# Constant fills on GpSimd, maxima of pairs as a reduction, and a planner with other delays, in a hybrid encoder layer

## The chip, the cores and the metric

The kernel runs on one core of one Trainium2 chip. The metric is the device time of one execution in microseconds (us). The core has five instruction queues that each run in order: TensorE (PE, with its weight loads shown apart as PEld), VectorE (DVE), ScalarE (ACT), GpSimd (POOL) and SyncE (SP, which here only issues DMAs). They meet through semaphores. Matmul results lie in eight PSUM banks of 128 x 512 f32.

## What is computed

One encoder layer over 1024 tokens of width 1024, in float32: two attention groups side by side, an output projection, and a gated feed-forward net (FFN) with a short convolution. Cut to what matters:

```python
hn = rms_norm(x, norm1_g)
proj = hn @ w_in                       # -> qa (512) | ka, va (128 each) | qb, kb, vb (512 each)
qa = apply_axial_rope(rms_norm(qa, qa_norm_g), tables)
ka = apply_axial_rope(rms_norm(ka, ka_norm_g), tables)
out_a = global_gqa_attention(qa, ka, va)             # 8 query heads, 2 key heads, dense softmax
out_b = dilated_mixture_attention(rms_norm(qb, qb_norm_g), rms_norm(kb, kb_norm_g), vb)
mixed = concat([rms_norm(out_a, outa_norm_g), rms_norm(out_b, outb_norm_g)])
x = x + mixed @ w_out
x = x + conv_ffn(rms_norm(x, norm2_g), w_up, conv_w, conv_b, w_down)
```

Mixer B's `dilated_mixture_attention` attends through three windows, (128, 1), (512, 4) and (2048, 16) as (width, step), with a distance penalty for each head.

## The kernel before

Numbers are kept as pairs of fp32r (a rounded value and the remainder), so most products are three matmuls, and most operands are made by a copy on ACT and a subtraction ("split") on DVE.

**Stages.** (1) Up to about 187 us: the projections, as 28 products `in_product(m)`, m = 0 to 27, four chunks of seven Strassen-like products. `w_prep(m)` (L694) makes the weights of a product, on DVE a sum and a split; `in_out(m)` adds the result to its chunk. Queries of mixer A go through the steps of `done`: `square`, `root` (with the four small instructions of `newton`), `norm`, `table` and four `turn`s of two rotations each on GpSimd, then `cos` and `add` on DVE. (2) Up to about 405 us: mixer A, 16 groups g of 128 queries by four heads (`a_prep(g)`, `a_main(g)`). (3) Up to about 545 us: mixer B, 8 heads h (`b_prep(h)`, `b_s`, `b_pv`). (4) The output projection, to about 566 us. (5) The FFN.

**The maxima.** The softmax subtracts a maximum over all the keys of a query. `mx(i)` in `a_prep` makes scores of one query block in two banks of PSUM by two matmuls; DVE reduces each bank to a column, into `SM_MC` + i for the first half and `SM_MC` + 8 + i for the second. `last` takes the larger of each pair for the four i at once, writes it into spare columns of the query's remainder, and PE turns these round by four transposes, with a copy by ACT behind. `trl(hf)` in `b_prep` does the same for mixer B. So there are 32 such 128x4 instructions, 16 in each mixer.

**The hand-over.** The first group's maxima (`a_prep(0)`: `nat`, `first`, four `mx`, `last`) are computed between the last products, 25 to 27, on two banks used in turn. So the matmuls of the second `mx` wait for the reductions of the first.

**Constants.** Columns of the operand tiles hold constants: ones and zeros in `R_VA` and `R_VB` beside the values, zeros in `R_QLN` and `R_QLB`, −1 in the lower half of `R_KHA` and of one key set. Before, each is filled by a DVE `tensor_scalar` that multiplies any finite tile by 0 and adds the constant; there are 18 instructions, from `fill` (L538), `fill_k` (L674) and the list `fills`.

**What sets the order.** No engine's order is the code's. The class `Recorder` (L124) notes each operation, finds its dependencies, and gives it a cost (`price`). `simulate` then runs the program with these costs as a list scheduler: at each step it takes the engine that can start first, and on it the ready operation with the most urgent due time, PE's operations by their number in the code. A PSUM bank is held until the last user's end and delay. DVE instructions with two SBUF operands (and copies and `tensor_scalar` within SBUF) and GpSimd's share a lock in this model: one waits for the other. `emit` issues the operations in the order of their planned starts; each engine's queue then has this order fixed. As every instruction is issued in `emit`, every row of the profile names L437 (L442 in the changed kernel).

Of the kernel before, what the change touches and what calls it, by code (L numbers as in the profile page):

```python
# [11 lines left out]
F32 = mybir.dt.float32  # L12
# [3 lines left out]
OP = mybir.AluOpType  # L16
# [107 lines left out]
class Recorder:  # L124


    TABLE = {"Sqrt": 1, "Exp": 2, "Gelu_apprx_tanh": 3}

    def __init__(self, nc):
# [182 lines left out]
    def simulate(self, order=None, window=400):  # L312

        n = len(self.ops)
        eng = [op[0] for op in self.ops]
        succs = [[] for _ in range(n)]
        for i, p in enumerate(self.preds):
            for j in p:
                succs[j].append(i)
        lag = lambda i, j: (120 if self.short[i] else 0) if eng[i] == eng[j] != 4 and self.ops[i][1] != "dma_start" else \  # L320
            self.cost[i][1] + (self.cost[i][3] if self.ops[i][1] == "dma_start" else 0)
        late = [0.0] * n
        nxt = 0.0
        for i in range(n - 1, -1, -1):
            c = self.cost[i][0]
            t = min([late[j] - lag(i, j) for j in succs[i]], default=0.0) - c
            if eng[i] == 0:
                t = min(t, nxt - c)
                nxt = t
            late[i] = t  # L330
        key = [float(i) if eng[i] == 0 else late[i] + (self.cost[i][3] if eng[i] == 4 else 0) for i in range(n)]
        if order is not None:
            key = order
        left = [len(p) for p in self.preds]
        ready = [0.0] * n
        avail = [[] for _ in range(5)]
        for i in range(n):
            if not left[i]:
                avail[eng[i]].append(i)
        free = [700.0] * 5  # L340
        held = [[0.0] * 5 for _ in range(8)]
        lock = fabric = 0.0
        table = 0
        start, done = [0.0] * n, 0
        seq = []
        queue = None
        if order is not None:
            queue = [sorted([i for i in range(n) if eng[i] == e], key=lambda i: order[i]) for e in range(5)]
            head = [0] * 5
        lowest = 0  # L350
        waiting = [False] * n
        issued = [False] * n
        pe = [i for i in range(n) if eng[i] == 0]
        pe_at = 0

        def when(e, j):
            t = max(free[e], ready[j], lock if self.cost[j][2] else 0.0)
            for b in self.banks[j]:
                for k in range(4):
                    if k != e and held[b][k] > t:  # L360
                        t = held[b][k]
            return t

        while done < n:
            best = None
            for e in range(5):
                if queue is not None:
                    if head[e] < len(queue[e]) and not left[queue[e][head[e]]]:
                        i = queue[e][head[e]]
                        t = max(free[e], ready[i])  # L370
                        if best is None or t < best[0]:
                            best = (t, e, i)
                    continue
                a = avail[e]
                if not a:
                    continue
                t = min(when(e, i) for i in a)
                if best is None or t < best[0]:
                    best = (t, e, None)
            t, e, i = best  # L380
            if i is None:
                a = [j for j in avail[e] if when(e, j) <= t + 1e-6]
                i = min(a, key=lambda j: key[j])
                if e == 0:
                    while issued[pe[pe_at]]:
                        pe_at += 1
                elif e != 4:
                    soon = [j for j in avail[e] if t < when(e, j) < t + self.cost[i][0] and key[j] < key[i]]
                    if soon:
                        j = min(soon, key=lambda j: when(e, j))  # L390
                        if key[i] - key[j] > 2 * (when(e, j) - t):
                            i, t = j, when(e, j)
            c = self.cost[i]
            if c[2]:
                t = max(t, lock)
            for b in self.banks[i]:
                t = max(t, *[held[b][k] for k in range(4) if k != e])
            if e == 1 and c[3] and c[3] != table and self.ops[i][1] == "activation":
                t += 1290
                table = c[3]  # L400
            start[i] = t
            issued[i] = True
            free[e] = t + c[0]
            if c[2]:
                lock = t + c[0]
            end = t + c[0]
            if self.ops[i][1] == "dma_start":
                fabric = max(end + 600, fabric) + c[3]
                land = fabric + c[1] - 600
            else:  # L410
                land = end + c[1]
            for b in self.banks[i]:
                held[b][e] = land
            seq.append(i)
            done += 1
            if queue is None:
                avail[e].remove(i)
            else:
                head[e] += 1
            for j in succs[i]:  # L420
                same = eng[j] == e and e != 4 and self.ops[i][1] != "dma_start"
                ready[j] = max(ready[j], end + (120 if self.short[i] else 0) if same else land)
                left[j] -= 1
                if not left[j] and queue is None:
                    avail[eng[j]].append(j)
        self.start, self.late = start, late
        return seq, max(free)
# [13 lines left out]
def tile_encoder_layer(ctx, tc, x, xt, w_kv, w_in, gains, outg, norm2_g, w_out, w_up, conv,  # L441
# [95 lines left out]

    def fill(dst, n, m, c):  # L538

        vec.tensor_scalar(dst, f(O_IDF, m)[:, None, :].to_broadcast([128, n, m]), 0.0, c, op0=OP.mult, op1=OP.add)  # L540

# [129 lines left out]

    def fill_k():  # L674
        for i in range(4):
            vec.tensor_scalar(r(R_KHA + 512 * i, 512)[64:128], f(F_ROPE, 512)[64:128], 0.0, -1.0,
                              op0=OP.mult, op1=OP.add)


    def w_buf(c, half):  # L680
# [209 lines left out]
    def a_prep(g):  # L890
# [17 lines left out]
                vec.tensor_reduce(f(SM_MC + 8 * hf + i, 1), bank(t), axis=AX.X, op=OP.max)  # L908

        def last():  # L910
            vec.tensor_tensor(rp(R_QLN + 512 * kv + 64, [128, 4]), f(SM_MC, 4), f(SM_MC + 8, 4), op=OP.max)
            t = next_tr()
            for i in range(4):
                tr_r(t, i, r(R_QLN + 128 * (4 * kv + i), 128))
# [89 lines left out]
    def b_prep(h):  # L1004
# [43 lines left out]

        def trl(hf):
            qln = R_QLB[h % 2]  # L1050
            vec.tensor_tensor(rp(qln + 64 + 512 * hf, [128, 4]), f(SM_MC + 4 * hf, 4), f(SM_MC + 8 + 4 * hf, 4),
                              op=OP.max)
            t = next_tr()
            for i in range(4):
# [185 lines left out]
            fills.append(lambda o=R_VB + 1024 * i + c, v=v: fill(rp(o, [256, 4], [1, 64]), 4, 64, v))  # L1240
    fills.append(lambda: fill(rp(R_QLB[1] + 64, [128, 8], [1, 64]), 8, 64, 0.0))
    for i in range(4):
        fills.append(lambda o=R_SET[0] + 2048 + 512 * i: vec.tensor_scalar(
            r(o, 512)[64:128], f(O_QAB, 512)[64:128], 0.0, -1.0, op0=OP.mult, op1=OP.add))

    def take(prep, n):
        for _ in range(n):
# [533 lines left out]
```

## Time and profile before

| | us |
|---|---|
| median of 3 runs (1293.58 to 1294.5) | 1294.02 |
| the profiled execution, its own time | 1292.44 |
| its span in the trace | 1290.7 |
| idle time of PE in the span | 20.7 |
| DVE busy | 1104.3 |
| ACT busy | 739.1 |
| POOL busy | 106.7 |

How to read the rows: an instruction's row has its start, its length, the engine, the operation, the tile written and the tiles read (`bigf` the f32 arena, `bigr` the fp32r arena, `ps` PSUM) and their shapes; in brackets stands the engine's idle time just before it, and what ended that. A group's row has the count, the busy time in us and the mean in ns, and behind the second bar the idle time before its members. The chain is followed back from the last instruction to what released each step.

### The profile page before, as it was taken

What the parts mean: (1) busy time and instruction counts of PE and PEld (TensorE: products, weight loads), DVE (VectorE), ACT (ScalarE), POOL (GpSimd) and SP (SyncE); (2) the same over time, 40 slices, a digit from 0 to 9 for tenths busy, and PEclk for the clock granted to TensorE, in tenths of its full rate; (3) what the DMA queues carried; (4) which work ended last, traced back from release to release, by engine and by line L of the source; (5) the groups of instructions that cost most, each with busy time, mean ns of one, the idle gap of its engine ahead of it and who ended that gap; (6) DMA issues with size and microseconds to landing.
All of it is one profiled execution on the core that took longest, in us unless ns stands there. A gap on an engine that the chain in (4) does not pass through costs nothing.

```text
span 1290.7 us, 19118 instructions
## 1 busy us (share of the span) xinstructions
PE 1270.0 (98%) x6916; PEld 1083.5 (84%) x6916; DVE 1104.3 (86%) x1924; ACT 739.1 (57%) x1192; POOL 106.7 (8%) x99
## 2 busy tenths in 40 slices
PE   7999989999999999999999999999999999999998
PEld 7999987887888888878888888888888888888887
DVE  6997799999997778798589999999999998876664
ACT  7865456998888767763455444444444444343331
POOL 0011042301101212000130000000000000000000
PEclk9999999999999999999999999999999999999999
DMA  8534211100003643452313223323322337976873
GB/s 333 176 75 115 83 39 42 31 1 1 9 1 93 150 117 92 119 180 98 98 61 103 90 75 115 115 97 123 119 79 81 122 139 255 329 262 220 278 244 108
DMA packets 118206, 156.99 MB, mean 122 GB/s; under 512 B 50656, under 2 KB 75744, under 8 KB 117088
## 3 DMA queue, kind: packets, MB, share of 16 engines
q1 hardware_dynamic: 116816, 152.36, 36.8%
q0 software_dynamic: 1152, 3.15, 0.9%
q8 instruction: 54, 0.88, 0.3%
q10 hardware_dynamic: 144, 0.27, 0.1%
q14 instruction: 40, 0.33, 0.1%
HBM read 117.73 MB, written 33.82 MB: 117 GB/s over the span
## 4 chain that ended last, share of the span: by engine, by line
PE 89%; DVE 7%; ACT 2%; DMA 1%; issue 1%; DVEq 0%; ACTq 0%; SPq 0%
PE ps L437 89%; DVE bigf L437 4%; DVE bigr L437 3%; ACT bigf L437 1%; ACT bigr L437 1%; DMA bigf<-w_in 0%; DMA bigf<-w_kv 0%; DMA bigf<-w_out 0%; ACT L437 0%; ACT ps L437 0%; DVEq L437 0%; ACTq L437 0%; SPq L437 0%
## 5 line engine op out<-in xcount | busy, mean ns | idle before, releaser
L437 PE MATMUL ps<-bigr 128*128 128x512 f32 (+3 forms) x6532 | 1239.3, 350 | 15.7 <-ACT bigr L437 6.6
L437 PEld LDWEIGHTS ps<-bigr 128*128 128x128 f32 x6532 | 1044.8, 187 | 188.8 <-ACT bigr L437 11.6
L437 ACT ACTIVATE bigr<-bigf 128x512 fp32r<-128x512 f32 (+2 forms) x358 | 270.6, 769 | 291.1 <-PE ps L437 217.9
L437 DVE TENSOR_TENSOR bigr<-bigf,bigr 128x512 fp32r<-128x512 f32 (+2 forms) x326 | 283.3, 880 | 49.5 <-ACT bigr L437 46.0
L437 DVE TENSOR_TENSOR bigf<-bigf 128x512 f32<-128x512 f32 (+3 forms) x298 | 216.4, 749 | 25.2 <-DMA bigf<-w_down 18.4
L437 DVE TENSOR_TENSOR bigf<-ps,bigf 128x512 f32<-128x512 f32 (+3 forms) x262 | 177.6, 686 | 47.4 <-PE ps L437 37.5
L437 ACT ACTIVATE bigr<-ps 128x512 fp32r<-128x512 f32 (+1 forms) x292 | 166.9, 602 | 84.5 <-PE ps L437 82.9
L437 ACT ACTIVATE bigf<-bigf 128x1024 f32<-128x1024 f32 (+5 forms) x186 | 142.6, 794 | 74.9 <-DVE bigf L437 58.4
L437 DVE SCALAR_TENSOR_TENSOR bigf<-bigf 128x255 f32<-128x255 f32 (+6 forms) x283 | 164.0, 596 | 9.0 <-ACT bigf L437 5.5
L437 DVE TENSOR_TENSOR bigr<-ps,bigr 128x512 fp32r<-128x512 f32 x188 | 126.9, 684 | 27.1 <-ACT ps L437 17.8
L437 ACT ACTIVATE ps<-ps 128x512 f32<-128x512 f32 x192 | 115.1, 601 | 9.2 <-PE ps L437 8.3
L437 ACT ACTIVATE bigf<-ps 128x512 f32<-128x512 f32 (+3 forms) x112 | 71.1, 637 | 68.1 <-PE ps L437 42.8
L437 DVE TENSOR_REDUCE bigf<-ps 128x1 f32<-128x512 f32 x128 | 81.3, 680 | 1.9 <-PE ps L437 1.7
L437 POOL TENSOR_TENSOR bigf<-bigf 128x128 f32<-128x128 f32 (+3 forms) x54 | 58.2, 1104 | 255.8 <-DVE bigf L437 255.5
L437 POOL TENSOR_TENSOR bigr<-bigf,bigr 128x512 fp32r<-128x512 f32 x32 | 43.9, 1376 | 288.3 <-ACT bigr L437 124.4
L437 PE MATMUL ps<-bigf 65*128 65x65 f32 (+2 forms) x384 | 62.8, 293 | 1.1 <-DVE bigf L437 1.1
L437 PEld LDWEIGHTS ps<-bigf 65*128 65x128 f32 (+2 forms) x384 | 43.7, 139 | 14.0 <-DVE bigf L437 1.9
L437 DVE CUSTOM_DVE_ANT_1 bigf<-ps,bigf 128x432 bf16<-128x432 f32 x64 | 38.6, 603 | 3.4 <-PE ps L437 3.0
L437 DVE CUSTOM_DVE_ANT_0 bigf<-ps,bigf 128x256 bf16<-128x256 f32 x64 | 26.9, 420 | 2.9 <-PE ps L437 2.4
L437 DVE TENSOR_REDUCE bigf<-bigf 128x16 f32<-128x1024 f32 x13 | 15.8, 1213 | 1.2 <-ACT bigf L437 1.2
L437 ACT ACT_TABLE_LOAD x11 | 14.1, 1283 | 1.7 <-PEq L1773 1.2
L437 DVE TENSOR_SCALAR bigr<-bigf 128x256 fp32r<-128x256 f32 (+2 forms) x22 | 8.7, 427 | 5.2 <-DMA bigf<-w_kv 5.1
(18 smaller groups left out, 66.9 us busy)
## 6 DMA issues: line engine op xcount, KB each, us to landing
bigf<-w_down SPq DMA_DIRECT2D x99, 256.0 KB, 3.9
bigf<-w_up SPq DMA_DIRECT2D x44, 512.0 KB, 3.6
bigf<-gscr SPq DMA_DIRECT2D x77, 256.0 KB, 3.8
gscr<-bigf SPq DMA_DIRECT2D x33, 512.0 KB, 3.9
bigf<-w_in SPq DMA_DIRECT2D x8, 1024.0 KB, 6.1
bigf<-x SPq DMA_DIRECT2D x16, 512.0 KB, 4.7
bigf<-tmx SPq DMA_DIRECT2D x8, 672.0 KB, 4.1
bigr<-bigr SPq DMA_DIRECT2D x16, 256.0 KB, 3.0
```

The costliest lines, as they stand in the source:

```text
L437: method(*args, **kw)
```

## The change

1. `fill`, `fill_k` and the four lambdas of `fills` become GpSimd memsets: 18 instructions leave DVE and 18 come on GpSimd.
2. `last` and `trl` take the maxima of pairs by `tensor_reduce` over one operand whose inner axis strides from the first half to the second, in place of `tensor_tensor` over two operands.
3. The planner's delays between engines come from a table `LAG` (rows PE, ACT, DVE, GpSimd; columns the waiting engine, SP last), where each engine had one figure; a bank's holder releases it after the delay to the engine that waits. Where two engines could start at the same time, the one whose operation is more urgent is planned first, which decides who takes the lock.

The number of operations is the same.

```diff
+    LAG = ((215, 200, 200, 200, 195), (150, 150, 140, 185, 157), (135, 122, 140, 168, 115), (150, 150, 150, 150, 80))
...
-        lag = lambda i, j: (120 if self.short[i] else 0) if eng[i] == eng[j] != 4 and self.ops[i][1] != "dma_start" else \
-            self.cost[i][1] + (self.cost[i][3] if self.ops[i][1] == "dma_start" else 0)
+        is_dma = [op[1] == "dma_start" for op in self.ops]
+
+        def lag(i, j):
+            if is_dma[i]:
+                return self.cost[i][1] + self.cost[i][3]
+            if eng[i] == eng[j]:
+                return 120 if self.short[i] else 0
+            return self.LAG[eng[i]][eng[j]]
...
-                    if k != e and held[b][k] > t:
-                        t = held[b][k]
+                    if k != e and held[b][k] + self.LAG[k][e] > t:
+                        t = held[b][k] + self.LAG[k][e]
...
-                t = min(when(e, i) for i in a)
-                if best is None or t < best[0]:
-                    best = (t, e, None)
-            t, e, i = best
+                t, k = min((when(e, i), key[i]) for i in a)
+                if best is None or (t, k) < best[:2]:
+                    best = (t, k, e, None)
+            t, _, e, i = best
...
-        vec.tensor_scalar(dst, f(O_IDF, m)[:, None, :].to_broadcast([128, n, m]), 0.0, c, op0=OP.mult, op1=OP.add)
+        gp.memset(dst.bitcast(F32), c)
...
-            vec.tensor_scalar(r(R_KHA + 512 * i, 512)[64:128], f(F_ROPE, 512)[64:128], 0.0, -1.0,
-                              op0=OP.mult, op1=OP.add)
+            gp.memset(rf(R_KHA + 512 * i, 512)[64:128], -1.0)
...
-            vec.tensor_tensor(rp(R_QLN + 512 * kv + 64, [128, 4]), f(SM_MC, 4), f(SM_MC + 8, 4), op=OP.max)
+            vec.tensor_reduce(rp(R_QLN + 512 * kv + 64, [128, 4]), fp(SM_MC, [1, 4], [8, 2]), axis=AX.X, op=OP.max)
...
-            vec.tensor_tensor(rp(qln + 64 + 512 * hf, [128, 4]), f(SM_MC + 4 * hf, 4), f(SM_MC + 8 + 4 * hf, 4),
+            vec.tensor_reduce(rp(qln + 64 + 512 * hf, [128, 4]), fp(SM_MC + 4 * hf, [1, 4], [8, 2]), axis=AX.X,
                               op=OP.max)
...
-        fills.append(lambda o=R_SET[0] + 2048 + 512 * i: vec.tensor_scalar(
-            r(o, 512)[64:128], f(O_QAB, 512)[64:128], 0.0, -1.0, op0=OP.mult, op1=OP.add))
+        fills.append(lambda o=R_SET[0] + 2048 + 512 * i: gp.memset(rf(o, 512)[64:128], -1.0))
```

Where instructions move. First DVE at the hand-over, before: the tail of a root with `newton` (RECIPROCAL to SCALAR_TENSOR_TENSOR) around the split of the weights of product 27, `norm`, fills (TENSOR_SCALAR), the sum of product 25 (`ps,bigf`, 128x1024), a split of values, a fill, and the reductions of the first two `mx`.

```order
L437 RECIPROCAL bigf<-bigf 128x16
L437 TENSOR_TENSOR bigf<-bigf 128x16
L437 TENSOR_TENSOR bigr<-bigf,bigr 128x1024
L437 SCALAR_TENSOR_TENSOR bigf<-bigf 128x16 x2
L437 TENSOR_TENSOR bigf<-bigf 128x4x256
L437 TENSOR_SCALAR bigr<-bigf 128x4x64 x2
L437 TENSOR_SCALAR bigr<-bigf 128x8x64
L437 TENSOR_SCALAR bigr<-bigf 128x4x64 x2
L437 TENSOR_TENSOR bigf<-ps,bigf 128x1024
L437 TENSOR_TENSOR bigr<-bigf,bigr 128x8x64
L437 TENSOR_SCALAR bigr<-bigf 128x8x64
L437 TENSOR_REDUCE bigf<-ps 128x1 x4
```

The same place now. The first row is the sum of the weights of product 27, `cos` and `add`; then come the sum of product 24, the split of the weights of product 27, the first group's `nat`, the sum of product 25, the reductions, and behind them the root's tail, `v_scale`, another `nat` and `newton`.

```order
L442 TENSOR_TENSOR bigf<-bigf 128x4x256 x3
L442 TENSOR_TENSOR bigf<-ps,bigf 128x4x256
L442 TENSOR_TENSOR bigr<-bigf,bigr 128x1024
L442 TENSOR_TENSOR bigr<-bigf,bigr 128x4x64
L442 TENSOR_TENSOR bigf<-ps,bigf 128x1024
L442 TENSOR_REDUCE bigf<-ps 128x1 x4
L442 SCALAR_TENSOR_TENSOR bigf<-bigf 128x16
L442 TENSOR_TENSOR bigf<-bigf 128x8x64 x2
L442 TENSOR_TENSOR bigr<-bigf,bigr 128x4x64
L442 RECIPROCAL bigf<-bigf 128x16
L442 TENSOR_TENSOR bigf<-bigf 128x16
L442 SCALAR_TENSOR_TENSOR bigf<-bigf 128x16 x2
```

What moved: `cos`, `add` and the sum of product 24 stood behind the four reductions and stand ahead of them; `newton`, `norm`, `v_scale` and the split of values stood ahead and stand behind; the fills are gone from this queue.

GpSimd at the same place, before: eight rotations (128x8x16) of one block of queries, `table` and eight rotations of the next, `table` of a third, then the `v_split` and the two table loads for mixer B.

```order
L437 TENSOR_TENSOR bigf<-bigf 128x8x16 x8
L437 TENSOR_TENSOR bigf<-bigf 128x4x128
L437 TENSOR_TENSOR bigf<-bigf 128x8x16 x8
L437 TENSOR_TENSOR bigf<-bigf 128x512
L437 TENSOR_TENSOR bigr<-bigf,bigr 128x8x64
L437 DMA bigr<-tbc 128x768 x2
```

And now, from behind the first eight rotations:

```order
L442 MEMSET bigr 64x512 x3
L442 TENSOR_TENSOR bigf<-bigf 128x4x128
L442 MEMSET bigr 64x512
L442 TENSOR_TENSOR bigf<-bigf 128x8x16 x8
L442 MEMSET bigr 128x4x64 x4
L442 TENSOR_TENSOR bigf<-bigf 128x512
L442 MEMSET bigr 128x8x64 x3
L442 TENSOR_TENSOR bigr<-bigf,bigr 128x8x64
L442 MEMSET bigr 64x512 x2
L442 MEMSET bigr 128x8x64 x2
L442 MEMSET bigr 64x512 x2
L442 DMA bigr<-tbc 128x768 x2
```

The rotations and splits keep their order among themselves, the memsets stand between them, four of them ahead of the second eight rotations (one more stands ahead of the first eight) and all of them ahead of the table loads.

In mixer B the order of DVE around a `trl` stays; only the instruction is another. Before (the ISA rows are reductions of scores by a custom instruction and the read of its result, the RECIPROCAL belongs to an output):

```order
L437 ISA bigf<-ps,bigf 128x256
L437 ISA bigf 128x1
L437 TENSOR_TENSOR bigr<-bigf 128x4
L437 RECIPROCAL bigf<-ps 128x4
L437 TENSOR_TENSOR bigr<-ps,bigr 128x512
```

And now:

```order
L442 ISA bigf<-ps,bigf 128x256
L442 ISA bigf 128x1
L442 TENSOR_REDUCE bigr<-bigf 128x4
L442 RECIPROCAL bigf<-ps 128x4
L442 TENSOR_TENSOR bigr<-ps,bigr 128x512
```

Nothing moved here beyond the maximum's own operation.

More of the change, by code (lines that the diff above doesn't have):

```diff
@@ L371, in simulate @@
                         if best is None or t < best[0]:
-                            best = (t, e, i)
+                            best = (t, 0.0, e, i)
                     continue
@@ L396, in simulate @@
             for b in self.banks[i]:
-                t = max(t, *[held[b][k] for k in range(4) if k != e])
+                t = max(t, *[held[b][k] + self.LAG[k][e] for k in range(4) if k != e])
             if e == 1 and c[3] and c[3] != table and self.ops[i][1] == "activation":
@@ L406, in simulate @@
             end = t + c[0]
-            if self.ops[i][1] == "dma_start":
+            land = end
+            if is_dma[i]:
                 fabric = max(end + 600, fabric) + c[3]
                 land = fabric + c[1] - 600
-            else:
-                land = end + c[1]
             for b in self.banks[i]:
-                held[b][e] = land
+                held[b][e] = end
             seq.append(i)
@@ L420, in simulate @@
             for j in succs[i]:
-                same = eng[j] == e and e != 4 and self.ops[i][1] != "dma_start"
-                ready[j] = max(ready[j], end + (120 if self.short[i] else 0) if same else land)
+                ready[j] = max(ready[j], land if is_dma[i] else end + lag(i, j))
                 left[j] -= 1
```

## The prediction, made before the changed kernel was run

> **What bounds the kernel now.** I read the profile's engine line first, then its chain, the chain in order of time, and engine time cut by stage.
>
> ```profile
> PE 1270.0 (98%) x6916; PEld 1083.5 (84%) x6916; DVE 1104.3 (86%) x1924; ACT 739.1 (57%) x1192; POOL 106.7 (8%) x99
> PE 89%; DVE 7%; ACT 2%; DMA 1%; issue 1%; DVEq 0%; ACTq 0%; SPq 0%
> 565.82 719.00 PE ps L437 x3226
> ```
>
> PE is busy 1270.0 of 1290.7 us and carries the chain except at a few places. No PE instruction is removed, so only the 20.7 us in which PE idles, and steps that run slowly beside them, can be won. The stage table says where they are (columns: length; busy time with instructions of PE, PEld, DVE, ACT and POOL; granted PE clock; DMA share; GB/s):
>
> ```profile
> 187.00:209.00 22.00, 17.49 (x107) 14.59 (x106) 20.57 (x33) 6.05 (x11) 1.26 (x2) 0.92 0.28 82
> 209.00:405.00 196.00, 195.93 (x985) 158.42 (x984) 184.43 (x359) 174.15 (x328) 32.74 (x30) 1.00 0.06 12
> 405.00:545.00 140.00, 135.90 (x1007) 119.95 (x1006) 111.77 (x347) 102.25 (x188) 27.76 (x25) 1.00 0.49 124
> 545.00:566.00 21.00, 19.89 (x112) 15.68 (x111) 19.48 (x38) 14.47 (x25) 0.00 (x0) 1.00 0.55 175
> 566.00:1285.00 719.00, 719.00 (x3228) 594.75 (x3227) 607.95 (x929) 320.99 (x456) 17.28 (x12) 1.00 0.43 146
> ```
>
> PE idles 22.00 − 17.49 = 4.51 us at the hand-over from projections to mixer A, 0.07 in mixer A, 4.10 in mixer B, 1.11 at the hand-over to the FFN, and nothing in the FFN's 719 us. The rest lies in the load at the start and in the last 5.7 us, where the change touches nothing. Two places can move: 187 to 209, and mixer B.
>
> **The hand-over to mixer A.** The timeline of PE, and the group of its weight loads from 186 to 209:
>
> ```profile
> 185.74 1.62 PE L437 MATMUL ps<-bigr 128*128 128x256 f32 x10
> 190.84 7.50 PE L437 MATMUL ps<-bigr 128*128 128x512 f32 x35 [3.48 <-DVE bigf L437]
> 198.98 0.38 PE L437 MATMUL ps<-bigr 128*128 128x256 f32 x1 [0.64 <-DVE bigf L437]
> L437 PEld LDWEIGHTS ps<-bigr 128*128 128x128 f32 x112 | 15.8, 203 | 7.5 <-DVE bigf L437 5.8 <-ACT bigr L437 0.5 <-DVE bigr L437 0.4
> ```
>
> PE stands 3.48 us before the second pair of mx matmuls: their two banks hold the first pair, which DVE has not reduced. DVE in that stretch:
>
> ```profile
> 177.07 0.68 DVE L437 TENSOR_TENSOR bigr<-bigf,bigr 128x256 fp32r<-128x256 f32 x1
> 177.76 0.59 DVE L437 TENSOR_SCALAR bigr<-bigf 64x512 fp32r<-64x512 f32 x1
> 178.36 0.34 DVE L437 SCALAR_TENSOR_TENSOR bigf<-bigf 128x16 f32<-128x16 f32 x1
> 178.63 1.55 DVE L437 TENSOR_TENSOR bigf<-bigf 128x512 f32<-128x512 f32 x2
> 180.21 1.78 DVE L437 TENSOR_SCALAR bigr<-bigf 64x512 fp32r<-64x512 f32 x3
> 182.02 0.25 DVE L437 RECIPROCAL bigf<-bigf 128x16 f32<-128x16 f32 x1
> 182.31 0.87 DVE L437 TENSOR_TENSOR bigf<-bigf 128x16 f32<-128x16 f32 x1
> ...
> 184.24 1.48 DVE L437 SCALAR_TENSOR_TENSOR bigf<-bigf 128x16 f32<-128x16 f32 x2
> 185.75 1.22 DVE L437 TENSOR_TENSOR bigf<-bigf 128x1024 f32<-128x1024 f32 x1
> 186.90 1.23 DVE L437 TENSOR_SCALAR bigr<-bigf 128x256 fp32r<-128x256 f32 x5
> ...
> 189.17 0.68 DVE L437 TENSOR_TENSOR bigr<-bigf,bigr 128x512 fp32r<-128x512 f32 x1
> 189.77 0.42 DVE L437 TENSOR_SCALAR bigr<-bigf 128x512 fp32r<-128x512 f32 x1
> 190.11 1.28 DVE L437 TENSOR_REDUCE bigf<-ps 128x1 f32<-128x512 f32 x2
> ```
>
> DVE never rests here, and the reduces start at 190.11 behind ten fills (the TENSOR_SCALAR rows): 0.59 + 1.78 + 1.23 + 0.42 = 4.02 us, which leave DVE. By the new order the root's tail, v_scale, newton, norm and a v split also go behind the reduces: 0.34 + 1.55 + 0.25 + 0.87 + 1.48 + 1.22 + 0.68 = 6.4. Ahead of them come cos, add and the sum of product 24, by this group's mean 3 × 1.22 = 3.7:
>
> ```profile
> L437 DVE TENSOR_TENSOR bigf<-bigf 128x1024 f32<-128x1024 f32 x68 | 82.3, 1223 | 0.7
> ```
>
> And cos waits for GpSimd's eight rotations:
>
> ```profile
> 158.51 3.67 POOL L437 TENSOR_TENSOR bigf<-bigf 128x128 f32<-128x128 f32 x8 [31.95 <-DVE bigf L437]
> 174.75 8.40 POOL L437 TENSOR_TENSOR bigf<-bigf 128x128 f32<-128x128 f32 x9 [6.58 <-DVE bigf L437]
> ```
>
> This is the wait that the change adds, and everything on DVE queues behind it, the reduces included. Beside DVE's additions nine of these took 8.40 us; beside a DVE that reduces or waits, eight took 3.67, 0.46 each. In the new order DVE still has two additions until 177.1, under which I let two rotations pass; then it waits, so the other six take 6 × 0.46 = 2.8 and end at 179.9. From there cos, add, sum 24, split 27 and sum 25 (5 × 1.22), with a quarter-size split (0.3 to 0.68), end at about 186.4. The reduces start 3.7 us earlier; the same by difference: −4.0 − 6.4 + 3.7 + 2.8 = −3.9.
>
> What PE gets: the first reduce ends near 187.1 and PE is through with its ten matmuls at 187.36, so of 3.48 I leave 0.4 for ScalarE's copy: **−3.1**. Sum 24 is done before the last product, so the 0.64 at 198.98 goes: **−0.6**. Of the other 0.39 of idle half: **−0.2**. The granted clock of 0.92 cost 8% of 17.49, 1.4 us; with the long pause gone I count back half to two thirds: **−0.8**. Together −4.7. Bounds: 4.51 + 1.4 = 5.9, with 0.6 more for slow weight loads, is −6.5 at best; if the rotations end at 181.7 as in the run before and a contended DVE step comes on top, 2.2 us go back: −2.5.
>
> Newton and norm, put behind, are late next; they feed the next block of queries, well behind the first scores. The fills that DVE gives up stand on GpSimd, which had this to offer for a price:
>
> ```profile
> L437 POOL MEMSET bigf<- 128x8 f32 x1 | 0.1, 113 | 0.1
> L437 POOL TENSOR_TENSOR bigr<-bigf,bigr 128x512 fp32r<-128x512 f32 x32 | 43.9, 1376 | 288.3 <-ACT bigr L437 124.4 <-ACT bigf L437 59.8 <-PE ps L437 54.4
> ```
>
> A memset of 512 is between 0.11 (of 8 elements) and 1.38 us (a 512-wide subtraction with two operands). I take 0.7, half of the subtraction's row, which is the nearest in size and streams two operands that a memset has not. GpSimd idles 6.58 us ahead of the rotations, and the four memsets put there take 0.4 to 5.5: cost nothing on the sum. Queued behind the later ones are the v split and two table loads, wanted in mixer B, 200 us on.
>
> **Mixer B.** The 32 pair maxima cost 0.17 us each, except here (all DVE instructions of that form in mixer B: min, median, max in ns):
>
> ```profile
> L437 DVE TENSOR_TENSOR bigr<-bigf x14: 166/167/1279, 414.8 to 535.5; 128x4 fp32r<-128x4 f32 x14
> 456.86 1.26 POOL L437 TENSOR_TENSOR bigr<-bigf,bigr 128x512 fp32r<-128x512 f32 x1 [7.11 <-PE ps L437]
> 456.86 1.28 DVE L437 TENSOR_TENSOR bigr<-bigf 128x4 fp32r<-128x4 f32 x1
> 458.29 0.93 PE L437 MATMUL ps<-bigr 128*128 128x128 f32 x7 [1.13 <-DVE bigr L437]
> ...
> 438.01 1.33 POOL L437 TENSOR_TENSOR bigr<-bigf,bigr 128x512 fp32r<-128x512 f32 x1 [7.05 <-PE ps L437]
> 438.02 0.17 DVE L437 TENSOR_TENSOR bigr<-bigf 128x4 fp32r<-128x4 f32 x1
> ...
> 478.22 0.93 PE L437 MATMUL ps<-bigr 128*128 128x128 f32 x7 [1.13 <-DVE bigr L437]
> ...
> 498.19 0.93 PE L437 MATMUL ps<-bigr 128*128 128x128 f32 x7 [1.13 <-DVE bigr L437]
> ```
>
> Three times a maximum starts at the instant of GpSimd's 512-wide subtraction and lasts as long as it does, 1.28 us, and PE waits 1.13 for it. At 438 GpSimd's instruction starts as close, and the maximum takes 0.17. So the second operand in SBUF is what GpSimd holds off. A reduction over one operand reads no second one; that it runs freely beside GpSimd is shown by these two rows, the second to be read with the rotations at 158.51 above:
>
> ```profile
> 158.20 1.21 DVE L437 TENSOR_REDUCE bigf<-bigf 128x16 f32<-128x1024 f32 x1
> L437 DVE TENSOR_REDUCE bigf<-bigf 128x16 f32<-128x1024 f32 x13 | 15.8, 1213 | 1.2 <-ACT bigf L437 1.2
> ```
>
> Gain 3 × (1.28 − 0.17) = **−3.3**, between −3.0 and −3.6 by the tail.
>
> Against this edit speaks a rule of the Trainium skill, "VectorE: DVE Perf Modes", section "Rules for kernel authors": a reduction is the slowest VectorE operation and should be restructured away. The rows deny it at width: 1213 ns for 1024 elements reduced, 1223 for the addition. Were the rule right by a factor of two here, 14 maxima at 0.17 more would leave −0.9 of the −3.3.
>
> **The rest.** In mixer A DVE is busy 184.43 of 196 us and the tie rule reshuffles many places, each a wait of a tenth at most as PE's 0.07 of idle shows; the FFN has no idle PE to win. I put −0.5 to +1.5 on it and take 0.
>
> **Sum.** −4.7 − 3.3 = −8.0. The profiled run took 1292.44 (its span of 1290.7 and 1.74 around it), which makes 1284.4; it lay 1.58 under the median of the runs, 1294.02, and against that median I predict 1286.0.
>
> **Rivals.**
> (a) The new wait replaces the old: the rotations end at 181.7 or later and ScalarE, which in the new order has copies that wait for add ahead of the copy that frees PE, holds the first transposes; the hand-over gives nothing. For it: nine rotations did take 8.40. Against: they were slow beside DVE's additions, which now wait themselves. Only mixer B's 3.3 is left: 1290.7.
> (b) The reduction meets GpSimd's hold all the same, or the new order makes new meetings in mixer B. For it: three of fourteen met by order alone. Against: the 158.20 row. Only the hand-over: 1289.3.
> (c) Nothing moves: PE's order there is hidden by later waits in mixer A, whose DVE is nearly full, and the meetings go on: 1294.0. Against it: PE's 0.07 of idle.
> (d) Slower: the memsets run at 1.38 us and hold off DVE as GpSimd's subtraction does. Twelve stand ahead of or among the rotations and the reduces: 12 × 1.38 = 16.6, on a DVE without rest; −8.0 + 16.6 = +8.6, 1302.6. It turns the sign when the rotations end 8 us late, after 188. For it: the 1.28 row shows GpSimd holding DVE. Against: a memset has no operand to read. The Trainium skill, "SBUF — State Buffer", section "Who interferes with whom", says that a VectorE instruction with two SBUF inputs contends with a GpSimd instruction that reads SBUF, not with one that only writes it; no run here shows a memset beside such an instruction yet. By that rule (d) falls away.
>
> **How the numbers follow.** Both terms, 72%: −2.5 − 3.0 + 1.5 = −4.0 to −6.5 − 3.6 − 0.5 = −10.6, so 1283.4 to 1290.0, likeliest 1286.0. (a) 11%, (b) 7%, (c) 5%, (d) 5%. The range 1283.4 to 1290.8 takes in (a) and (b). A measurement of this kernel tells 0.2%, 2.6 us, from no change; faster is below 1291.4. (a) lies just there, so I give 4 of its 11 to no change: faster 0.86, same 0.09, slower 0.05.
>
> **What would show it.** From 187 to 209: PE idle under 1.5 us, clock near 1.00, the first reduces near 186.5, rotations ending near 180. In mixer B: 128x4 reductions with a maximum under 0.3 us, PE idle near 0.8. On GpSimd: memsets under 1.4 us, no DVE step stretched beside one. I am wrong if DVE waits for GpSimd beyond 182, if a 128x4 reduction lasts over a microsecond, or if idle of PE in mixer A exceeds 2 us.

## The result

| kernel | median, us | runs | lowest to highest |
|---|---|---|---|
| before | 1294.03 | 6 | 1292.45 to 1294.76 |
| changed | 1284.55 | 6 | 1284.07 to 1285.81 |

The ratio is 0.9929, with a 95% interval of 0.9916 to 0.9941: 9.5 us off, clear of the 0.2% that can be told apart. 1286.0 was predicted, with 1283.4 to 1290.8 around it.

### The profile after

The engine line and the chain on the page of the changed kernel:

```profile
PE 1269.3 (99%) x6916; PEld 1080.9 (84%) x6916; DVE 1084.5 (84%) x1906; ACT 741.0 (58%) x1192; POOL 112.0 (9%) x117
PE 89%; DVE 4%; DMA 4%; ACT 1%; issue 1%; SPq 0%; ACTq 0%; DVEq 0%
```

And the stages that held the idle time (columns as before):

```profile
187.00:209.00 22.00, 21.91 (x138) 18.72 (x137) 21.28 (x38) 11.41 (x22) 4.24 (x8) 1.00 0.29 86
209.00:405.00 196.00, 195.72 (x997) 156.97 (x995) 179.88 (x352) 176.10 (x330) 32.61 (x30) 1.00 0.08 20
405.00:545.00 140.00, 138.58 (x1021) 122.03 (x1020) 114.50 (x355) 104.08 (x188) 27.73 (x25) 1.00 0.47 118
```

PE's idle time from 187 to 209 went from 4.51 to 0.09 us, its clock there from 0.92 to 1.00, and the idle time from 405 to 545 from 4.10 to 1.42. The two windows do not hold quite the same work, as the changed kernel is further on at 545; between the same instructions of mixer B (the landmarks below) PE's idle time went from 4.69 to 1.42. The span is 1284.0, and the profiled execution took 1285.81, the slowest of the six; that of before, 1292.44, was the fastest of its six. So the two profiles are only 6.6 us apart, the medians 9.5.

The share of DVE in the chain fell from 7% to 4%; that of DMA rose from 1% to 4%, as the chain now runs through loads of the residual that end at 1131 us (more of this below). Rows of GpSimd, DVE and PE at the hand-over, in the changed kernel's timeline:

```profile
174.50 5.23 POOL L442 TENSOR_TENSOR bigf<-bigf 128x128 f32<-128x128 f32 x8 [5.54 <-DVE bigf L442]
...
175.40 1.48 DVE L442 TENSOR_TENSOR bigf<-bigf 128x1024 f32<-128x1024 f32 x1
...
179.76 2.48 DVE L442 TENSOR_TENSOR bigf<-bigf 128x1024 f32<-128x1024 f32 x2 [2.87 <-POOL bigf L442]
...
186.49 19.81 PE L442 MATMUL ps<-bigr 128*128 128x512 f32 x125 [0.17 <-ACT bigr L442]
...
187.03 2.68 DVE L442 TENSOR_REDUCE bigf<-ps 128x1 f32<-128x512 f32 x4 [1.05 <-PE ps L442]
```

The forecast's picture is all there: DVE stands 2.87 us for the rotations, which end at 174.50 + 5.23 = 179.73, and yet PE's wait of 3.48 is 0.17. The reductions, which PE waited for, now wait for PE. PE's weight loads from 186 to 209, 203 ns in the mean before:

```profile
L442 PEld LDWEIGHTS ps<-bigr 128*128 128x128 f32 x140 | 19.5, 186 | 3.7 <-ACT bigr L442 0.7 <-DVE bigf L442 0.7 <-DVE bigr L442 0.4
```

In mixer B, all its 128x4 maxima (min, median and max in ns), and from the timeline one that meets GpSimd:

```profile
L442 DVE TENSOR_REDUCE bigr<-bigf x14: 162/164/167, 409.2 to 526.8; 128x4 fp32r<-128x8 f32 x14
```

```profile
451.41 1.29 POOL L442 TENSOR_TENSOR bigr<-bigf,bigr 128x512 fp32r<-128x512 f32 x1 [7.10 <-PE ps L442]
451.41 0.16 DVE L442 TENSOR_REDUCE bigr<-bigf 128x4 fp32r<-128x8 f32 x1
```

Same start to the hundredth, and no hold. The memsets by form, and from the timeline two of them beside two-operand additions:

```profile
L442 POOL MEMSET bigr<- 64x512 f32 x8 | 4.0, 522 | 6.8 <-PE ps L442 6.7
L442 POOL MEMSET bigr<- 128x512 f32 x6 | 3.0, 529 | 31.4 <-PE ps L442 31.4
L442 POOL MEMSET bigr<- 128x256 f32 x4 | 1.2, 318 | 0.7 <-PE ps L442 0.6
```

```profile
163.59 1.23 DVE L442 TENSOR_TENSOR bigr<-bigf,bigr 128x1024 fp32r<-128x1024 f32 x1 [0.41 <-ACT bigr L442]
164.27 0.98 POOL L442 MEMSET bigr<- 64x512 f32 x2 [2.17 <-PE ps L442]
164.73 1.22 DVE L442 TENSOR_TENSOR bigf<-bigf 128x1024 f32<-128x1024 f32 x1
```

The additions last 1.22 and 1.23 as they do alone (1223 ns in the mean): these memsets hold nobody.

### Stage by stage

To compare traces whose starts differ, take the same PE instructions in each: the last matmul of product 25, the last of product 27, the first score of mixer B's second head, the last matmul of its eighth, the last of the FFN. Differences of their times, in us, from one profile each. The column of mixer A runs on into mixer B's first head.

| kernel | hand-over | mixer A | mixer B | after mixer B |
|---|---|---|---|---|
| before | 21.71 | 215.72 | 132.92 | 732.86 |
| changed | 15.23 | 216.27 | 129.77 | 734.53 |
| before_again | 22.03 | 215.70 | 134.09 | 733.57 |
| maxima_only | 22.41 | 215.74 | 129.48 | 733.39 |
| fills_only | 16.75 | 215.93 | 135.26 | 732.91 |
| planner_only | 16.03 | 221.81 | 134.19 | 735.61 |
| after_again | 15.23 | 216.37 | 129.77 | 734.21 |
| both_old_order | 16.77 | 215.84 | 129.59 | 732.93 |
| both_replanned | 14.55 | 215.42 | 129.28 | 733.07 |
| tie_off | 14.66 | 216.17 | 129.76 | 732.91 |
| tie_only | 16.50 | 215.87 | 129.31 | 732.63 |
| two_operands_back | 15.23 | 217.69 | 134.06 | 733.13 |
| rotations_1us_late | 17.47 | 216.37 | 129.70 | 733.19 |
| rotations_3us_late | 21.73 | 216.22 | 129.68 | 733.42 |

The changed kernel: −6.5 at the hand-over, +0.6 in mixer A, −3.2 in mixer B, +1.7 behind it.

The hand-over column does not hold the same work in all rows. In the order of before (before, before_again, maxima_only, fills_only, both_old_order) ten 128x512 matmuls of PE stand between the two landmarks, in all the other plans eight; the other two follow behind product 27 and count in mixer A. Without its idle time the stretch takes 15.75 in fills_only, with ten, and 15.05 in the changed kernel, with eight. So about 0.7 of the −6.5 is work that moved, and it accounts for the +0.6 in mixer A: like for like the hand-over gave −5.8 and mixer A nothing.

### The profile page after: what moved, and what is told of

It is laid out like the page before. It is cut to its first block, busy times and chain, and to the rows that moved or that the text cites. A ratio compares the mean times of both kernels' runs of the same rounds, so it can differ in the third digit from the quotient of the medians.

```text
span 1284.0 us, 19129 instructions
## 1 busy us (share of the span) xinstructions
PE 1269.3 (99%) x6916; PEld 1080.9 (84%) x6916; DVE 1084.5 (84%) x1906; ACT 741.0 (58%) x1192; POOL 112.0 (9%) x117
## 4 chain that ended last, share of the span: by engine, by line
PE 89%; DVE 4%; DMA 4%; ACT 1%; issue 1%; SPq 0%; ACTq 0%; DVEq 0%
PE ps L442 89%; DVE bigr L442 2%; DVE bigf L442 2%; DMA bigf<-rscr 1%; ACT bigr L442 1%; DMA bigf<-gscr 1%; DMA gscr<-bigf 0%; DMA bigf<-w_down 0%; DMA bigf<-w_out 0%; DMA bigf<-w_kv 0%; ACT L442 0%; SPq L442 0%; ACT bigf L442 0%; ACT ps L442 0%; ACTq L442 0%
## 5 line engine op out<-in xcount | busy, mean ns | idle before, releaser
L442 PEld LDWEIGHTS ps<-bigr 128*128 128x128 f32 x6532 | 1042.7, 187 | 183.5 <-ACT bigr L442 13.2
L442 DVE SCALAR_TENSOR_TENSOR bigf<-bigf 128x255 f32<-128x255 f32 (+5 forms) x283 | 162.5, 590 | 8.4 <-ACT bigf L442 4.9
L442 PE MATMUL ps<-bigf 128*128 128x128 f32 (+2 forms) x384 | 63.0, 294 | 1.4 <-DVE bigf L442 1.3
L442 PEld LDWEIGHTS ps<-bigf 128*128 128x128 f32 (+2 forms) x384 | 43.3, 140 | 15.1 <-DVE bigf L442 2.5
L442 POOL MEMSET bigr<- 64x512 f32 (+2 forms) x18 | 8.2, 479 | 39.0 <-PE ps L442 38.8
```

The source lines that it names most:

```text
L442: method(*args, **kw)
```

## The experiments

Each ran beside the kernel before on the same chip. That kernel's median was 1295.76, 1295.64 and 1292.37 in the three groups below. As that kernel's own time turns out to vary from run to run, by what before_again shows, its median moves the ratios too; where groups differ, the stage table is the safer comparison.

### Each part alone

**before_again**: no edit. 

> The kernel before once more, for a second profile. Theory (race): a two-operand maximum that meets GpSimd's 512-wide subtraction is held for its whole length or not at all by which of the two starts first, within some 10 ns, so the count of maxima over 1 us among the six meetings need not be 3 again, and each one more or less moves the time by 1.1 us; that would be why single runs spread over 2.3 us. Rival (fixed): the order decides, 3 of 6 are long in this profile too, and the spread is elsewhere. Both: PE idle about 4.5 us from 187 to 209.

Measured: 1295.29 (11 runs, 1291.21 to 1297.87), ratio 0.9996 (0.9984 to 1.0008). Two meetings in its timeline:

```profile
438.88 1.29 POOL L437 TENSOR_TENSOR bigr<-bigf,bigr 128x512 fp32r<-128x512 f32 x1 [7.06 <-PE ps L437]
438.89 1.31 DVE L437 TENSOR_TENSOR bigr<-bigf 128x4 fp32r<-128x4 f32 x1
...
440.35 0.82 PE L437 MATMUL ps<-bigr 128*128 128x128 f32 x6 [1.17 <-DVE bigr L437]
498.79 1.34 POOL L437 TENSOR_TENSOR bigr<-bigf,bigr 128x512 fp32r<-128x512 f32 x1 [7.11 <-PE ps L437]
498.79 0.17 DVE L437 TENSOR_TENSOR bigr<-bigf 128x4 fp32r<-128x4 f32 x1
```

In the first profile the meeting at 438 was short and that at 496.76 long; here the first is long and the later one short. Four of six are held in place of three. It is a race, decided within the trace's hundredth of a microsecond, and each loss costs PE 1.1 to 1.2 us. The sixth meeting is none:

```profile
537.48 0.17 DVE L437 TENSOR_TENSOR bigr<-bigf 128x4 fp32r<-128x4 f32 x1
537.48 1.33 POOL L437 TENSOR_TENSOR bigr<-bigf,bigr 128x512 fp32r<-128x512 f32 x1 [18.07 <-ACT bigr L437]
```

Here GpSimd waits for ScalarE and DVE starts first, by 0.005 to 0.007 us in the trace; in all five profiles of kernels with two operands it was not held. At the other five places DVE's start stands 0.005 to 0.008 behind GpSimd's, whether it is held or not.

**maxima_only**: every queue in the order of before, the reduction priced to the planner as the old instruction.

```diff
-            vec.tensor_tensor(rp(R_QLN + 512 * kv + 64, [128, 4]), f(SM_MC, 4), f(SM_MC + 8, 4), op=OP.max)
+            vec.tensor_reduce(rp(R_QLN + 512 * kv + 64, [128, 4]), fp(SM_MC, [1, 4], [8, 2]), axis=AX.X, op=OP.max)
```

> The kernel before with the 32 maxima as one-operand reductions, every queue's order as before. Theory: mixer B loses PE's three waits of 1.13, the 128x4 reductions that meet GpSimd last 0.17, the hand-over stays: -3.3 us on the profile (1289.1), and -3.3 to -5 on the median if other runs of the kernel before had four or five long maxima. Rival: the reduction is held too: 0. Rival: the gain is lost again behind mixer B (waits at the output projection): -1 or less.

Measured: 1290.34 (5 runs), ratio 0.9961 (0.9948 to 0.9973). Its maxima in mixer B:

```profile
L439 DVE TENSOR_REDUCE bigr<-bigf x16: 154/164/166, 398.6 to 533.5; 128x4 fp32r<-128x8 f32 x16
```

Mixer B takes 129.48 in place of 132.92, −3.4; the hand-over gains nothing (22.41). Only the instruction differs, so the gain is the instruction's. On the median it is 5.4 us; that other runs of the kernel before lose more than three races would explain it, but the races of the timed runs are in no trace.

**fills_only**: the fills as memsets, planned at DVE's old price and place and issued on GpSimd, so that what is left in every queue keeps its order.

```diff
+    def set_to(dst, c, like):
+        rec.ops.append((2, "memset", nc.gpsimd.memset, (dst.bitcast(F32), c), {"_like": like}))
...
-        vec.tensor_scalar(dst, f(O_IDF, m)[:, None, :].to_broadcast([128, n, m]), 0.0, c, op0=OP.mult, op1=OP.add)
+        set_to(dst, c, f(O_IDF, m)[:, None, :].to_broadcast([128, n, m]))
```

> The kernel before with the 18 fills as GpSimd memsets at their planned place, all other queues in the order of before. Theory (fills one to one): DVE's reductions at the hand-over start 4.0 us earlier, at 186.1, PE's wait of 3.48 goes down to under 0.5 and the later waits shrink: -4 to -6 us. Rival (order needed): taken without the new order, DVE waits for something else there (GpSimd's rotations, ScalarE's copies): -2 or less. Rival (memsets hold DVE): DVE instructions with two SBUF operands last longer than 1.23 us beside a memset, 0 to +3.

Measured: 1289.22 (5 runs), ratio 0.9950 (0.9936 to 0.9963). DVE and PE at the hand-over, in its timeline:

```profile
185.78 7.22 PE L437 MATMUL ps<-bigr 128*128 128x256 f32 x51
...
187.34 2.59 DVE L437 TENSOR_REDUCE bigf<-ps 128x1 f32<-128x512 f32 x4 [0.81 <-PE ps L437]
...
193.24 1.10 PE L437 MATMUL ps<-bigr 128*128 128x512 f32 x2 [0.23 <-DVE bigf L437]
195.01 11.32 PE L437 MATMUL ps<-bigr 128*128 128x256 f32 x72 [0.67 <-DVE bigf L437]
```

PE's long wait is gone without any new order, and the reductions wait for PE; only 0.23 and the 0.67 before product 27 are left. The hand-over takes 16.75 in place of 21.71, −5.0. DVE's small steps ahead of the reductions became shorter too, as the rotations no longer run beside them (`newton`'s 0.87 takes 0.18), but that was not needed: the trace is 1.0 later at the last of product 25, and 190.11 + 1.0 − 4.0 = 187.1 is where the reductions start, within 0.25. Mixer B lost all five races in this profile (135.26), and still the median is 6.5 us lower.

**planner_only**: the delay table and the tie rule, with fills on DVE and maxima of two operands.

```diff
-        gp.memset(dst.bitcast(F32), c)
+        vec.tensor_scalar(dst, f(O_IDF, m)[:, None, :].to_broadcast([128, n, m]), 0.0, c, op0=OP.mult, op1=OP.add)
```

(and so on for the other fills and both maxima) 

> The kernel before with the new delays and tie rule alone; fills stay on DVE, maxima with two operands. Theory (order is a second way): cos, add and the sum of product 24 go ahead of the reductions and newton, norm and v_scale behind, with 1.0 us of fills still ahead; the reductions start near 187.2 and the hand-over gives -5 to -6; the maxima may meet GpSimd in up to six places, so mixer B gives +3.3 to -3.3: in all -2 to -8. Rival (fills carry it): DVE stays late at the hand-over, -2 or less there.

Measured: 1295.88 (11 runs), ratio 1.0001 (0.9992 to 1.0010). The hand-over did go to 16.03, −5.7 as expected (0.7 of it work that moved), and mixer A from 215.72 to 221.81: 6.1 us given back. Where, by its timeline from 254 to 283, and by the group of DVE's row sums in mixer A:

```profile
254.57 6.26 POOL L442 TENSOR_TENSOR bigf<-bigf 128x1024 f32<-128x1024 f32 x3
259.64 1.22 DVE L442 TENSOR_TENSOR bigr<-bigf 128x4 fp32r<-128x4 f32 x1
260.91 0.85 PE L442 MATMUL ps<-bigr 128*128 128x128 f32 x5 [1.09 <-DVE bigr L442]
277.53 2.41 PE L442 MATMUL ps<-bigr 128*128 128x512 f32 x8 [0.85 <-DVE bigr L442]
...
280.21 1.95 PE L442 MATMUL ps<-bigr 128*128 128x512 f32 x7 [0.27 <-DVE bigr L442]
...
282.79 1.44 PE L442 MATMUL ps<-bigr 128*128 128x512 f32 x5 [0.63 <-DVE bigr L442]
```

```profile
L442 DVE TENSOR_REDUCE bigf<-bigf 128x16 f32<-128x1024 f32 x4 | 4.9, 1220 | 0.4 <-ACT bigf L442 0.2
```

One maximum meets GpSimd in mixer A too, 1.09. The other three waits fall among these four row sums, 1.22 each, which the plan puts on DVE within 10 us (from 273.31 to 282.14), between the subtractions that PE needs; that they are the cause was read from the trace, not tried, and the changed kernel has three such sums from 269.18 to 275.12 where PE hardly waits (0.10 from 269 to 289). The four waits add up to 2.8. PE also ran slower between them (columns as in the stage table):

```profile
249.00:269.00 20.00, 18.91 (x93) 15.11 (x92) 19.82 (x31) 16.11 (x32) 14.80 (x21) 1.00 0.10 24
269.00:289.00 20.00, 18.04 (x76) 11.67 (x74) 18.67 (x35) 18.12 (x30) 3.10 (x2) 1.00 0.06 14
```

The kernel before does 100 and 101 matmuls in these two stretches; 32 fewer at 0.2 us each are about the whole loss. So the place is shown and the cause stays open. The forecast had "−2 to −8"; it did not see mixer A.

### The two edits together, and the planner apart

**after_again**: the changed kernel, no edit. 

> The changed kernel once more, beside the next three on one chip. Both theories: the six maxima that meet GpSimd in mixer B last 0.16 each, the hand-over idles under 0.3 us; 0.989 to 0.993 of the kernel before. Open: whether PE's waits of 0.37 and 0.79 us at 1130 us, on a transfer of the residual, come again; if they do, they belong to the change, if not, to that run.

Measured: 1285.29 (4 runs), ratio 0.9919 (0.9905 to 0.9932). The wait at 1130 came again, smaller. The hand-over and mixer B repeat to the hundredth, 15.23 and 129.77: no reduction is held there.

**both_old_order**: maxima_only and fills_only in one. 

> Fills on GpSimd and maxima as reductions, the order of every queue held as before (maxima_only and fills_only together). Theory (two edits, the planner adds little): the two gains add, -5.0 at the hand-over and -3.4 in mixer B (more in runs with more than three long maxima), about -8.4 us from the kernel before's profile, 1284.0, within 1.5 us of the changed kernel. Rival (the planner carries part): over 2 us slower than the changed kernel.

Measured: 1285.22 (5 runs), ratio 0.9921 (0.9907 to 0.9934), level with the changed kernel. −4.9 at the hand-over and −3.3 in mixer B, as each alone: by the stages the two add. The medians do not quite: 5.4 and 6.5 alone against the kernel before of their group, 10.4 together against that of this group. The kernel before's races may make the difference; that is not shown.

**both_replanned**: the changed kernel with the planner of before.

```diff
-            return self.LAG[eng[i]][eng[j]]
+        lag = lambda i, j: (120 if self.short[i] else 0) if eng[i] == eng[j] != 4 and self.ops[i][1] != "dma_start" else \
+            self.cost[i][1] + (self.cost[i][3] if self.ops[i][1] == "dma_start" else 0)
...
-                t, k = min((when(e, i), key[i]) for i in a)
+                t = min(when(e, i) for i in a)
```

> The changed kernel with the planner of before: fills on GpSimd, maxima as reductions, one delay for each engine and no tie rule, so the plan is made anew. Theory: cos and add go ahead of the first reductions here too and newton as well, the sums of products 24 and 25 behind; GpSimd's rotations are split by four memsets, the reductions start by 185.5 to 187; hand-over -4.5 to -6.5, mixer B -3.4: within 2 us of the changed kernel. Rival (the new delays matter): a wait of over 1 us comes back at the hand-over, or over 2 us are lost in mixer A.

Measured: 1282.74 (4 runs, 1282.54 to 1283.01), ratio 0.9899 (0.9886 to 0.9913): below every run of after_again on the same chip (1284.34 to 1286.07), and the fastest version of this study. DVE and PE at the hand-over, in its timeline:

```profile
183.75 3.56 DVE L437 TENSOR_TENSOR bigf<-bigf 128x1024 f32<-128x1024 f32 x2 [1.83 <-POOL bigf L437]
183.78 18.22 PE L437 MATMUL ps<-bigr 128*128 128x256 f32 x136
...
187.24 2.71 DVE L437 TENSOR_REDUCE bigf<-ps 128x1 f32<-128x512 f32 x4
```

PE runs through the whole hand-over without a wait, 14.55. DVE waits for GpSimd here too, 1.83, but the copy that PE needs does not stand behind it.

**tie_off**: the changed kernel with the delay table, without the tie rule.

```diff
-                t, k = min((when(e, i), key[i]) for i in a)
-                if best is None or (t, k) < best[:2]:
-                    best = (t, k, e, None)
+                t = min(when(e, i) for i in a)
+                if best is None or t < best[0]:
+                    best = (t, 0.0, e, None)
```

> The changed kernel without the tie rule, the delays of the new table kept. Its order at the hand-over reads as that of both_replanned, so the tie rule and not the delays puts the sums ahead of the reductions and newton behind. Theory: as both_replanned within 1 us. Rival (delays matter elsewhere): over 1 us from it, by mixer A.

Measured: 1283.70 (4 runs), ratio 0.9907 (0.9894 to 0.9921); 14.66 at the hand-over, 216.17 in mixer A. It is 0.96 above both_replanned, just inside the 1 us, and 1.6 below after_again; 0.6 of that is the hand-over, 1.3 lies behind mixer B.

**tie_only**: the tie rule with the delays of before. 

> Fills on GpSimd, maxima as reductions, the planner with the tie rule but with the delays of before: the fourth of the four combinations. The sums of products 24 and 25 stand ahead of the first reductions as in the changed kernel. Theory (the tie rule costs the 1.6 to 2.5 us by which the changed kernel is behind tie_off and both_replanned): 1284.5 to 1286, with a loss in mixer A of 0.5 or more. Rival (the delays cost it, or the two together): within 1 us of both_replanned, 1282.7.

Measured: 1284.94 (6 runs), ratio 0.9934 (0.9923 to 0.9946), in the third group; 16.50 at the hand-over. The median is in the expected range, but the two groups' kernels before differ by 3.3 us, and by the ratios it is 4.5 us behind both_replanned. By the stage table it is 2.0 behind, all of it at the hand-over. Of the four planners the two with the tie rule take 15.2 and 16.5 there, the two without 14.55 and 14.66, with eight 512-wide matmuls in each. The loss that was expected in mixer A is not there (215.87).

### What can go wrong

**two_operands_back**: the changed kernel's order, maxima with two operands. 

> The changed kernel with the 32 maxima by two operands again, every queue's order as in the changed kernel. By the changed kernel's trace nine of them meet GpSimd: three while GpSimd is well inside its instruction (two in mixer A, with 1.1 and 0.8 us to go, one at the start of mixer B with 0.2), one 0.16 us after its start, five within 0.01 us of it. Theory: the first four are held to GpSimd's end, the five are held or not by chance; PE pays 1.1 for each of mixer B's: +2 to +7 us on the changed kernel, likeliest +4. Rival (the order keeps them apart): under +1.

Measured: 1290.54 (12 runs, 1289.02 to 1293.38), ratio 0.9984 (0.9973 to 0.9995). Mixer A takes 1.4 us more, mixer B 4.3: of its four races three were lost, and the meeting 0.14 us behind GpSimd's start as well; where DVE starts first it was not held. By the stage table that is 4.5 us more than after_again in all, close to the likeliest 4. The spread of its runs is 4.4 us, that of the changed kernel 1.7.

**rotations_1us_late** and **rotations_3us_late**: two and six memsets more behind the second rotation, issued in `emit`.

```diff
                 method(*args, **kw)
+                if i == mark[1]:
+                    for _ in range(2):
+                        self.pause()
```

> The changed kernel with two more memsets of 64x512 on GpSimd (constants written over themselves) between the second and third of the eight rotations; nothing else moves. They take 0.46 each in a row, so the rotations end 0.9 us later, near 180.6, and DVE's wait grows from 2.87 to 3.8. In the changed kernel DVE then idles 1.05 us once more, for PE's matmuls, ahead of the first reduction. Theory: that is the slack of the added wait; 0.9 fits in, the hand-over's PE idle stays under 0.5, the time within 0.5 us of the changed kernel. Rival (the wait is critical at once): +0.9.

> The same with six memsets: the rotations end 2.8 us later, near 182.5. Theory (slack of 1.05, then one to one): the first reduction starts 1.7 us later than in the changed kernel, PE waits 1.5 to 2 us more at the hand-over and the time is 1.5 to 2 us longer. Rival (critical at once): +2.8. Rival (much slack): under +0.5.

Measured: 1287.17 (4 runs), ratio 0.9954 (0.9938 to 0.9969), and 1291.27 (10 runs), ratio 0.9986 (0.9977 to 0.9996). Rows of three timelines: ScalarE in the changed kernel, DVE and PE with two memsets, ScalarE and PE with six.

```profile
182.28 0.63 ACT L442 ACTIVATE bigr<-bigf 128x512 fp32r<-128x512 f32 x1 [1.98 <-DVE bigf L442]
...
184.90 1.54 ACT L442 ACTIVATE bigr<-ps 128x512 fp32r<-128x512 f32 x3
```

```profile
180.76 3.46 DVE L443 TENSOR_TENSOR bigf<-bigf 128x1024 f32<-128x1024 f32 x2 [4.14 <-POOL bigf L443]
...
188.47 17.75 PE L443 MATMUL ps<-bigr 128*128 128x512 f32 x116 [2.42 <-ACT bigr L443]
```

```profile
187.00 0.63 ACT L443 ACTIVATE bigr<-bigf 128x512 fp32r<-128x512 f32 x1 [6.55 <-DVE bigf L443]
...
189.62 1.54 ACT L443 ACTIVATE bigr<-ps 128x512 fp32r<-128x512 f32 x3
...
191.21 14.96 PE L443 MATMUL ps<-bigr 128*128 128x512 f32 x96 [4.74 <-ACT bigr L443]
```

The hand-over takes 17.47 and 21.73 in place of 15.23, +2.2 and +6.5: more than either theory or any rival had. The theory of a slack of 1.05 fell. PE does not wait through DVE's reductions but through ScalarE: its queue has a copy of `add`'s result (182.28) ahead of the copy of the first transposes (184.90), which PE's `mx` reads. So DVE's wait for the rotations reaches PE at once: 2.42 in place of 0.17. With two memsets the rotations end 1.3 later against PE's work, with six 3.6, and the wait grows on the way, because `cos` and `add` now meet GpSimd's next table and take 3.46 in place of 2.48. The 1.05 us in which DVE idled were the same wait seen from the other side. Six memsets make it 4.74, more than PE idled there in the kernel before (4.30 between the same landmarks), with a clock of 0.84. So with rotations that end at 183.5 the whole gain of the hand-over is gone (21.73 against 21.71), and the median of 1291.27, on another chip, lies near the 1290.7 that the forecast gave its rival (a).

## Why the prediction was right

- **What bounds the kernel** (PE, at two places): right. Nearly all of the gain lies at these two.
- **The fills leave DVE, 4.02 us, and the reductions start earlier**: right, and shown by itself in fills_only, −5.0. That the memsets cost nothing held too; 0.7 was taken for one, 0.52 was measured. What was left open, whether they hold DVE, is answered by the additions beside them (1.22 and 1.23). The Trainium skill's rule ("SBUF — State Buffer", "Who interferes with whom") that GpSimd contends only when it reads agrees with these rows, and rival (d) falls.
- **The rotations and the added wait**: six rotations at 0.46 behind DVE's two additions were to end at 179.9 and ended at 179.73; the wait was put at 2.8 and was 2.87. One reading was off: the row of nine at 8.40 us, which rival (a) calls nine rotations, holds eight that ended at 181.7 and the `table` behind them (1.48).
- **The size of the hand-over** was the term that was off: −4.7 forecast, −6.5 by the landmarks, −5.8 like for like. The idle part was booked at 3.1 + 0.6 + 0.2 = 3.9; between the landmarks PE idled 4.30 before and 0.17 after, so it gave 4.1. The slow steps beside the pauses were booked at 0.8 of a possible 2.0. Without the idle time the stretch took 17.4 before and 15.75 in fills_only, with the same matmuls: 1.7. In the changed kernel, with no long pause, the clock was 1.00 and a weight load took 186 ns in the mean, against 203.
- **Mixer B**: −3.3 forecast, −3.2 in the profile, −3.4 in maxima_only. The Trainium skill's rule on reductions ("VectorE: DVE Perf Modes", "Rules for kernel authors") would have made them dearer; at this size the median is 164 ns against 167. That the kernel before tosses a coin at five of its six meetings was not seen; the profile it was argued from had lost three, the second one lost four, fills_only five. This may be why the medians moved by 9.5 where the sum said 8.0; the races of the timed runs themselves are in no trace.
- **The rest at 0**: right for mixer A, whose +0.6 is the two matmuls that moved. The part behind mixer B gave back 1.7 in this profile, 1.2 of it at 1130 us, where PE waits for work that stands behind loads of the residual. This came again at half the size in after_again and not in two_operands_back and the two runs with late rotations, which have the same order. That stays open.
- **That 1284.55 came so near 1286.0** is in part luck. Profile against profile the gain is 6.6, less than the 8.0 of the sum: the hand-over gave 1.1 more than booked, 1.7 went behind mixer B, where 0 was booked, and 0.7 ahead of the hand-over and behind the last matmul. Median against median it is 9.5, more than the sum.
- **Rival (a)** was the near miss. Its chain, DVE behind the rotations and PE's copy on ScalarE behind DVE, exists exactly as described; the rotations only came in time. The forecast's bounds allowed for it (−2.5 at worst); that the wait has no slack at all, and that rotations 3.6 us later would take the whole gain, came out only when they were delayed.
- **What the forecast did not ask** is which of the three edits it rested on. It argued the hand-over from the new order, and the order is not needed: both_old_order is level with the changed kernel. Its own sum for the reductions had the answer: −4.0 for the fills, and −6.4 + 3.7 + 2.8 = +0.1 for all that the order does. The delays and the tie rule give nothing alone (1.0001) and cost some 2.5 us beside the other two edits (1285.29 against 1282.74). Of this the hand-over is shown: the two plans with the tie rule take 0.6 to 2.0 us longer there. By the stage table after_again loses 0.7 to both_replanned at the hand-over, 1.0 in mixer A, 0.5 in mixer B and 1.1 behind it; what costs the last three was not tried.

## What to carry to other kernels

Where one engine's instruction can hold up another's and one of them is tiny, give it an operand form that is not held (here one operand in place of two): the price is not its own 0.17 us but the length of whatever the other engine is doing, and it comes at random. Constants belong on an engine that idles, when the engine that sets the pace has no rest there. Test a planner's new rules apart from the edits that come with them: here the good news of two edits hid a loss in the third.

## What was not expected of the hardware

- A race between DVE and GpSimd, where DVE's start stands 0.005 to 0.008 us behind, goes either way from run to run: 3, 4, 5 and 4 of five such maxima in mixer B were held in four profiles of kernels with two operands, 3 of four in two_operands_back, none in those with one.
- DVE, when it loses, waits to the end of GpSimd's instruction (1.18 to 1.31 us in mixer B); when DVE wins, GpSimd's takes 1.32 to 1.34 in place of 1.26 to 1.29.
- A GpSimd memset of 512 f32 took 0.52 us on 64 partitions as on 128, one of 256 took 0.32.
